# Loading the first tile of a row-norm kernel with two DMAs, one of the even and one of the odd partitions

## Chip, cores, metric

The kernel runs on one core of a Trainium2 chip. The metric is the device time of one execution in microseconds (us); lower is better. A profile is one execution; its span is some 1.8 us shorter than the device time.

## The reference

The input is 8192 x 8192 float32, 268 MB; the output is the largest absolute value of each row.

```python
def reference(x):
    return np.linalg.norm(x, ord=np.inf, axis=1)
```

Every byte is read once and reduced once, so the time cannot fall below that of the reading.

## The kernel before

The first 6144 rows go through as 24 tiles of 128 partitions with 64 KB each (two rows of the matrix per partition), with three buffers. The last rows are cut into smaller loads so that little work is left after the last byte. All loads are issued by SyncE (SP in the profile); VectorE (DVE) reduces.

```python
for a in range(A):                 # A = 6
    for n in range(G):             # G = 4
        t = sbuf.tile([P, W + PAD], F32, tag="t")      # 3 buffers, W = 16384
        nc.sync.dma_start(out=t[:, :W], in_=x_b[a, n])
        absmax(
            r_bulk[:, a, n * B : (n + 1) * B],
            t[:, :W].rearrange("p (b c) -> p b c", b=B),
        )
# ... 34 smaller loads and their reduces, two stores ...
nc.at_finalize(start_first_load_early)
nc.at_finalize(finish_on_pool)
```

`start_first_load_early` moves the first DMA of SyncE, and only that one, to the head of the program, before the start-up barrier of the engines. This move is called the hoist below:

```python
if ins.engine == sp and type(ins).__name__ == "InstDMACopy":
    assert not ins.sync_info.on_wait
    # ... taken out of its block and put in front of SyncE's first instruction
    return
```

Of the kernel before, what the change touches and what calls it, by code (L numbers as in the profile page):

```python
# [34 lines left out]
def segments(loads, cols):  # L35

    out, at = [], 0
    for i, w in enumerate(loads):
        end = at + w
        while at < end:  # L40
            r = at // cols
            to = min(end, (r + 1) * cols)
            out.append((i, r, at - r * cols, to - at))
            at = to
    return out
# [53 lines left out]
@with_exitstack  # L99
def kernel(  # L100
    ctx: ExitStack,
    tc: tile.TileContext,
    x: bass.AP,
    out: bass.AP,
    G: int = 4,
    B: int = 2,
    BUFS: int = 3,
    PAD: int = 16,
):
    nc = tc.nc  # L110
    P = nc.NUM_PARTITIONS
    rows, cols = x.shape
    W = B * cols


    n_tail = B * (len(TAIL) + 1)
    n_bulk_rows = rows // P - n_tail
    assert n_bulk_rows % (G * B) == 0
    A = n_bulk_rows // (G * B)
    split = n_bulk_rows * P  # L120
    x_b = x[:split].rearrange("(a p n b) c -> a n p (b c)", p=P, a=A, n=G, b=B)
    out_b = out[:split].rearrange("(a p n b) -> p a (n b)", p=P, a=A, n=G, b=B)
    x_t = x[split:].rearrange("(p t b) c -> t p (b c)", p=P, b=B)
    out_t = out[split:].rearrange("(p t) -> p t", p=P)

    sbuf = ctx.enter_context(tc.tile_pool(name="sbuf", bufs=BUFS))
    outp = ctx.enter_context(tc.tile_pool(name="outp", bufs=1))

    segs = [segments(loads, cols) for loads in TAIL]
    k_max = max(sum(r == b for _, r, _, _ in s) for s in segs for b in range(B))  # L130
    parts_of = [sum(r == b for r, _ in LAST) - 1 for b in range(B)]
    assert sum(parts_of) <= PAD

    r_bulk = outp.tile([P, A, G * B], F32)
    r_tail = outp.tile([P, n_tail], F32)
    part = outp.tile([P, n_tail - B, k_max], F32)
    nc.vector.memset(part[:], 0.0)  # L137

    def absmax(o, i):
        return nc.vector.reduce_max(  # L140
            out=o, in_=i, axis=X, apply_absolute_value=True
        )

    for a in range(A):
        for n in range(G):
            t = sbuf.tile([P, W + PAD], F32, tag="t")
            nc.sync.dma_start(out=t[:, :W], in_=x_b[a, n])
            absmax(
                r_bulk[:, a, n * B : (n + 1) * B],
                t[:, :W].rearrange("p (b c) -> p b c", b=B),  # L150
            )

    for i, loads in enumerate(TAIL):
        t = sbuf.tile([P, W + PAD], F32, tag="t")
        todo = segs[i]
        seen = [0] * B
        at = 0
        for j, w in enumerate(loads):
            nc.sync.dma_start(out=t[:, at : at + w], in_=x_t[i][:, at : at + w])  # L159
            at += w  # L160
            for _, b, c, n in [s for s in todo if s[0] == j]:
                k, lo = seen[b], b * cols + c
                absmax(part[:, i * B + b, k : k + 1], t[:, lo : lo + n])
                seen[b] += 1

    def after(ins, first, kind):
        info = mybir.DependencyInfo(kind, mybir.DependencyReason.SCHED_ONLY)
        tc.add_manual_dep(ins.ins, first.ins.name, info, reason="order")


    t = sbuf.tile([P, W + PAD], F32, tag="t")
    left = parts_of[:]
    col = [0] * B
    at, slot = 0, {}
    ends = [w for _, w in LAST[-B:]]
    lo = W - sum(ends)
    for b in range(B):
        slot[b] = lo + ends[b]
        lo = slot[b] + parts_of[b]
    for j, (b, w) in enumerate(LAST):  # L180
        final = left[b] == 0
        to = slot[b] - w if final else at
        frm = b * cols + col[b]
        nc.sync.dma_start(out=t[:, to : to + w], in_=x_t[len(TAIL)][:, frm : frm + w])
        col[b] += w
        if final:
            r = n_tail - B + b
            absmax(r_tail[:, r : r + 1], t[:, to : slot[b] + parts_of[b]])
        else:
            left[b] -= 1  # L190
            k = slot[b] + left[b]
            done = absmax(t[:, k : k + 1], t[:, to : to + w])
            at += w
        if j == 0:

            ins = absmax(r_tail[:, : n_tail - B], part[:])
            after(ins, done, mybir.DependencyClass.NoSync)
        if j == len(LAST) - 4:

            ins = nc.scalar.dma_start(out=out_b, in_=r_bulk[:])  # L200
            after(ins, done, mybir.DependencyClass.Sync)
    nc.sync.dma_start(out=out_t, in_=r_tail[:])
    nc.at_finalize(start_first_load_early)
    nc.at_finalize(finish_on_pool)
# [30 lines left out]
```

## Time and profile before

| | before |
|---|---|
| device time, median of 3 | 627.47 us (627.43 to 627.56) |
| span of the profile | 625.7 us |
| DMA rate over the span | 429 GB/s |
| one full tile of 8.39 MB | 19.35 us |
| VectorE busy | 552.9 us, 88% |
| first reduce begins | 21.99 us |

The prediction below shows the lines for most of this and reads them: the kernel is as long as the start of a stream of loads, the stream, and a short tail. Three words are used all through. A packet is one record of a DMA engine at work; for the big tiles it is one row of 64 KB. The completion write is the 4-byte record, of 0.009 us, that each of the 16 engines shows at the end of its part of a load (944 of them in SyncE's queue, for 58 loads and a store). A tile is called landed here when the last of the 16 is written.

From the timeline of the kernel before (start us, length us, queue, line, operation): the first load is issued in 0.38 us.

```profile
0.00 0.38 SPq L147 DMA_DIRECT2D t<-in_x_dram  x1
```

The view of the load's source line, with shortest, median and longest issue in ns over its 24 loads: an issue of 128 rows usually takes 0.328 us. (The longest, 0.632, is the third, which follows directly on the second.)

```profile
L147 SPq DMA_DIRECT2D t<-in_x_dram x24: 327/328/632, 0.0 to 425.9; - x24
```

### The profile page before, as it was taken

What the parts mean: (1) busy time and instruction counts of PE and PEld (TensorE: products, weight loads), DVE (VectorE), ACT (ScalarE), POOL (GpSimd) and SP (SyncE); (2) the same over time, 40 slices, a digit from 0 to 9 for tenths busy, and PEclk for the clock granted to TensorE, in tenths of its full rate; (3) what the DMA queues carried; (4) which work ended last, traced back from release to release, by engine and by line L of the source; (5) the groups of instructions that cost most, each with busy time, mean ns of one, the idle gap of its engine ahead of it and who ended that gap; (6) DMA issues with size and microseconds to landing.
All of it is one profiled execution on the core that took longest, in us unless ns stands there. A gap on an engine that the chain in (4) does not pass through costs nothing.

```text
span 625.7 us, 205 instructions
## 1 busy us (share of the span) xinstructions
DVE 552.9 (88%) x67; POOL 0.2 (0%) x4
## 2 busy tenths in 40 slices
DVE  0588988889988889888898888988889999999998
POOL 0000000000000000000000000000000000000000
DMA  9999999999999999999999999999999999999997
GB/s 402 469 402 452 419 452 419 448 423 436 436 419 452 411 461 402 469 402 469 402 469 402 461 411 452 419 448 423 444 413 421 444 425 431 436 425 430 424 422 315
DMA packets 9282, 268.49 MB, mean 429 GB/s; under 512 B 1856, under 2 KB 1856, under 8 KB 3392
## 3 DMA queue, kind: packets, MB, share of 16 engines
q1 hardware_dynamic: 8496, 268.45, 99.5%
q10 hardware_dynamic: 784, 0.02, 0.1%
q14 instruction: 2, 0.02, 0.0%
HBM read 268.44 MB, written 0.03 MB: 429 GB/s over the span
## 4 chain that ended last, share of the span: by engine, by line
DMA 67%; DVE 31%; issue 1%; another core or an unknown queue 0%; DVEq 0%; SPq 0%
DMA t<-in_x_dram 67%; DVE r_bulk L140 24%; DVE part L140 6%; DVE t L140 2%; DVEq L230 0%; DVE r_tail L140 0%; SPq L159 0%
## 5 line engine op out<-in xcount | busy, mean ns | idle before, releaser
L140 DVE TENSOR_REDUCE r_bulk<-t 128x2 f32<-128x16384 f32 x24 | 413.3, 17220 | 69.7 <-DMA t<-in_x_dram 69.7
L140 DVE TENSOR_REDUCE part<-t 128x1 f32<-128x8192 f32 (+20 forms) x28 | 121.5, 4410 | 0.3 <-DMA t<-in_x_dram 0.3
L140 DVE TENSOR_REDUCE t<-t 128x1 f32<-128x1664 f32 (+8 forms) x11 | 16.7, 1576 | 0.2 <-DMA t<-in_x_dram 0.2
L140 DVE TENSOR_REDUCE r_tail<-t 128x1 f32<-128x644 f32 (+1 forms) x2 | 1.5, 814 | 0.0
L137 DVE MEMSET part<- 128x56 f32 x1 | 0.1, 105 | 0.9 <-PEq L219 0.9
L140 DVE TENSOR_REDUCE r_tail<-part 128x14 f32<-128x56 f32 x1 | 0.2, 201 | 0.0
L219 POOL MEMSET const-bfloat16-1.0<- 128x1 bf16 x1 | 0.1, 101 | 0.0
L219 POOL MEMSET const-uint8-127<- 128x1 uint8 x1 | 0.1, 101 | 0.0
L219 POOL MEMSET const-float32-0.0<- 128x1 f32 x1 | 0.1, 98 | 0.2 <-issue 0.2
L219 POOL MEMSET const-float32-1.0<- 128x1 f32 x1 | 0.1, 98 | 0.0
## 6 DMA issues: line engine op xcount, KB each, us to landing
t<-in_x_dram SPq DMA_DIRECT2D x2, 3392.0 KB, 37.2
t<-in_x_dram SPq DMA_DIRECT2D x1, 5376.0 KB, 40.5
t<-in_x_dram SPq DMA_DIRECT2D x1, 4864.0 KB, 32.9
t<-in_x_dram SPq DMA_DIRECT2D x1, 4800.0 KB, 32.9
t<-in_x_dram SPq DMA_DIRECT2D x1, 4672.0 KB, 34.7
t<-in_x_dram SPq DMA_DIRECT2D x3, 1536.0 KB, 36.9
t<-in_x_dram SPq DMA_DIRECT2D x1, 3520.0 KB, 42.7
t<-in_x_dram SPq DMA_DIRECT2D x1, 3328.0 KB, 40.4
```

Of the source, the lines that this page charges most:

```text
L137: nc.vector.memset(part[:], 0.0)
L140: return nc.vector.reduce_max(out=o, in_=i, axis=X, apply_absolute_value=True)
L219: nc = _bacc.Bacc("TRN2", target_bir_lowering=False, num_devices=1)
```

## The change

The first load is what is issued first and what the whole stream stands behind. The change issues it as two loads of 64 partitions each. As the text of the change gives no reason, the intent is inferred: a smaller first DMA might be under way sooner.

```diff
             t = sbuf.tile([P, W + PAD], F32, tag="t")
-            nc.sync.dma_start(out=t[:, :W], in_=x_b[a, n])
+
+            step = 2 if a == n == 0 else 1
+            for k in range(step):
+                nc.sync.dma_start(out=t[k::step, :W], in_=x_b[a, n][k::step, :])
             absmax(
```

With a step of 1 the other 23 loads are what they were. The early-start pass moves only the even half.

## The prediction

> **What bounds the kernel now.** I read the page from the top: engine busy time, the DMA row over the span, the bytes, then the chain of waits, the waits of VectorE and of the issuing queue, and last the first microseconds in narrow windows.
>
> First the page's busy shares of the DMA engines over 40 slices and the bytes:
>
> ```profile
> span 625.7 us, 205 instructions
> DMA  9999999999999999999999999999999999999997
> ...
> HBM read 268.44 MB, written 0.03 MB: 429 GB/s over the span
> ```
>
> The DMA row is at 9 in every slice but the last. VectorE does much less than the span: its costliest group takes 17.22 us for a tile, and each time stands idle before it for a DMA:
>
> ```profile
> L140 DVE TENSOR_REDUCE r_bulk<-t 128x2 f32<-128x16384 f32 x24 | 413.3, 17220 | 69.7 <-DMA t<-in_x_dram 69.7
> ```
>
> The chain that ended last, in order of time, shows the period. (One step is called "an unknown queue"; it is the wait for a load.)
>
> ```profile
> 0.79 40.47 DMA t<-in_x_dram
> ...
> 60.64 17.23 DVE r_bulk L140
> 77.87 0.02 issue
> 77.89 40.76 DMA t<-in_x_dram
> 118.65 0.02 issue
> 118.67 17.23 DVE r_bulk L140
> 135.91 0.02 issue
> 135.92 40.77 DMA t<-in_x_dram
> ```
>
> Three tiles take 135.91 - 77.87 = 58.04 us, 19.35 us each. A tile is 128 rows of 64 KB, 8.39 MB, so 8.39 MB / 19.35 us = 434 GB/s. The chain passes through VectorE only because a reduce gives a buffer back. A load is then asked for with about two tiles (40.76 us) still ahead of its landing, so the queue never runs dry. This is a stream bounded by the DMA engines. The trace's records of single packets say the same: a 64 KB packet takes 2.418 us almost without exception. 8 rows on each of 16 engines make 8 x 2.418 = 19.34 us, the period. Everything after the first load is that stream; what can move is when it begins and how the first 8 MB flow.
>
> The first microseconds, in windows (columns: length, VectorE, GpSimd, clock, DMA share, GB/s; a packet's bytes stand in the window in which it starts):
>
> ```profile
> 0.50:1.00 0.50, 0.10 (x1) 0.00 (x0) 1.00 0.00 0
> 1.00:1.20 0.20, 0.00 (x0) 0.00 (x0) 1.00 9.39 3277
> 1.20:1.40 0.20, 0.00 (x0) 0.00 (x0) 1.00 1.90 655
> 1.40:1.60 0.20, 0.00 (x0) 0.00 (x0) 1.00 1.98 655
> 1.60:1.80 0.20, 0.00 (x0) 0.00 (x0) 1.00 0.96 328
> 1.80:2.00 0.20, 0.00 (x0) 0.00 (x0) 1.00 0.90 328
> ```
>
> One 64 KB packet in 0.2 us is 328 GB/s, so these windows hold 10, 2, 2, 1 and 1 packets, 16 in all, one for each engine. The packet records give the first start at 1.01 us after the issue and the last at 1.82 us. Those first packets take 2.80 to 3.23 us in place of 2.42. The spread stays: the 16 completion writes of the first tile lie from 20.74 to 21.61 us (0.87 us apart), those of the 24th bulk tile from 465.32 to 466.22 (0.90), and a load near 604 us still 0.94. All engines carry equal shares at an equal pace, so whoever starts last lands last in every tile, nearly to the end.
>
> [...]
>
> **The change part by part.**
>
> - It removes one 128-row load and adds two 64-row loads of the same bytes: 64 + 64 packets of 64 KB, still 8 an engine. Data time: 8 x 2.418 = 19.34 us before and after. Sum: 0.
> - It adds one issue on the SyncE queue. An issue takes 0.33 us (the median of the 24 loads of the bulk; the longest took 0.63). By then the engines have the first half: 4 x 2.418 = 9.7 us of work, and the second half is asked for about 1 to 1.5 us in. Hidden, 0. The next two loads are issued 0.3 us later, with some 19 us of work ahead of them: 0.
> - It adds one completion write on each engine. A record of one takes 0.009 us, and the next row starts within 0.01 us of its due time. Sum: +0.01 us.
> - VectorE's first reduce has two completions to wait for; both belong to the same stream. [...] 0.
> - It moves the start. Only the first SyncE load is hoisted to the head of the program, and that is now half as large. If the 0.81 us between first and last engine (1.01 to 1.82) is the writing of descriptors engine after engine, half the descriptors need half the time: the last engine starts 0.4 us earlier and, as the spread is carried to the end, so does the end. If the spread is something else (cold first accesses: the late starters had the shorter first packets), the gain is 0. The late starters' second packets begin 0.89 us after the earliest, so most of the spread is real lateness. I choose somewhat over half: -0.28 us.
>
> Sum: 627.47 - 0.28 + 0.01 = 627.2 us. That is 0.04%, and far under the 2% line.
>
> **The rivals.**
>
> [...] every packet takes 2 x 2.418 = 4.84 us, each half 19.3 us in place of 9.7, and the first tile 38.7. As the stream is never idle later, the 19.3 us are never given back: 627.2 + 19.3 = 646.5 us, +3.0%, slower. [...] I give it 16%.
>
> *False order.* The two loads write one buffer. If their rows are taken as overlapping (0 to 126 against 1 to 127), the second half waits for the first to land. The stream would then start twice: the first tile's reduce began at 21.99 us, 21.99 - 19.34 = 2.65 us of start in it, and about that is added: 630 us, +0.4%, within 2%. Against: partition steps are part of an access, and a tracker that has them sees no overlap. 4%.
>
> *Hidden anyway.* The spread has a fixed cause, the start does not move: 627.4 to 627.6. For it: three of the five earliest starters had packets over 3.1 us, so a cold start may level what the earlier start wins. About 30%.
>
> **Range and chances.** Gain and hidden cases together have some 80%: 626.9 to 627.6, widened to 626.4 to 628.4 for a larger start effect (a whole 0.8 us gone) or a small cost of the extra load that I have overlooked. The conflict lies outside of the range, and so does the false order. Faster by 2% would need 12.5 us, nearly five times the whole start: 1%. Slower by 2% needs the conflict: 16%. Within: 83%.
>
> **What would show each step.** Right: the first reduce still waits for the load until 21.6 to 21.9 us (21.99 before); the first-tile packets at 2.42 us after the first; the windows of 1.0 to 2.0 us again with 16 packets, but closer together; the completion spread of all later tiles nearer to 0.5 than 0.87; the period still 19.35; the queue with one more issue and VectorE's 69.7 us of idle time changed by less than 1. Wrong by conflict: the first reduce at about 41 us, first-tile packets of 4.84 us, GB/s near 217 in the first two slices, VectorE's idle time up by 19. Wrong by false order: a gap of no packets near 11 us and the first reduce near 24.6. If neither shows and the time is off by over 1 us, something that I have not named moved the end of the stream.

The sum is 627.47 - 0.28 + 0.01 = 627.2 us; VectorE's further wait counted as 0 in it. The first rival supposes that every packet of the first tile takes twice its 2.418 us, and the text calls it the conflict. Other estimates rest on suppositions too. That 64 rows run on all 16 engines, 4 on each, the trace after shows; that the spread of 0.81 us is the writing of descriptors, or cold first accesses, no record shows.

## The result and the profile after

The changed kernel took 628.22 us in the median of 6 runs (627.84 to 628.80); the kernel before, in the same rounds, took 627.53 us (627.43 to 627.70). The ratio is 1.0011 with a 95% interval from 0.9998 to 1.0024, so by the 2% line it is the same. A ratio here is the mean time of one kernel's runs over that of the other's of the same rounds, and so not quite the ratio of the medians. The time lies in the stated range (626.4 to 628.4), but the small difference has the wrong sign: a gain of 0.28 us at the start, 0.27 in sum, was forecast, and the median rose by 0.69.

The page of the changed kernel shows a machine that does the same as before. The DMA row is unchanged, and so is the rate; one more load and one more wait of VectorE have joined the instructions; VectorE's idle time in front of its large reduces is 69.9 us in place of 69.7.

```profile
span 626.5 us, 207 instructions
...
DMA  9999999999999999999999999999999999999997
...
HBM read 268.44 MB, written 0.03 MB: 429 GB/s over the span
...
L140 DVE TENSOR_REDUCE r_bulk<-t 128x2 f32<-128x16384 f32 x24 | 413.3, 17220 | 69.9 <-DMA t<-in_x_dram 69.9
```

The timeline of the changed kernel tells how long SyncE took over its first issue, the even half, and when the first reduce began:

```profile
0.00 0.56 SPq L150 DMA_DIRECT2D t<-in_x_dram  x1
...
22.36 17.22 DVE L140 TENSOR_REDUCE r_bulk<-t 128x2 f32<-128x16384 f32 x1 [20.96 <-DMA t<-in_x_dram]
```

Half the rows took 0.56 us to issue where all of them took 0.38, and the first reduce began at 22.36 us, 0.37 later than before. The narrow windows of the changed kernel (length, VectorE, GpSimd, clock, DMA share, GB/s) show the same at the DMA engines:

```profile
1.00:1.20 0.20, 0.00 (x0) 0.00 (x0) 1.00 0.00 0
1.20:1.40 0.20, 0.10 (x1) 0.00 (x0) 1.00 3.85 1311
1.40:1.60 0.20, 0.00 (x0) 0.00 (x0) 1.00 6.61 2294
1.60:1.80 0.20, 0.00 (x0) 0.00 (x0) 1.00 1.97 655
1.80:2.00 0.20, 0.00 (x0) 0.00 (x0) 1.00 1.87 655
2.00:2.20 0.20, 0.00 (x0) 0.00 (x0) 1.00 0.92 328
```

At 328 GB/s a packet these are 0, 4, 7, 2, 2 and 1 packets. Before, ten packets started between 1.0 and 1.2 us; now none does. The records of single packets put the first at 1.35 us (1.01 before) and the last engine's first at 2.09 (1.82 before): both ends of the start moved later, by 0.33 and 0.27 us, and the spread between them shrank by only 0.07. Of the two ends only the first repeats: in further profiles the last engine's first packet came at 2.40 us before, and at 2.01 and 2.14 with the change.

The chain that ended last, in order of time, has a new link, the issue of the second half, and then the old rhythm:

```profile
1.21 0.48 SPq L150
1.69 0.05 issue
1.74 39.85 DMA t<-in_x_dram
...
78.23 0.02 issue
78.25 40.87 DMA t<-in_x_dram
119.11 0.02 issue
119.13 17.23 DVE r_bulk L140
136.37 0.02 issue
136.38 40.80 DMA t<-in_x_dram
```

The new link need not cost time: when the second half has been issued, at 1.69 us, the engines have 4 rows of the first half each, over 9 us of work (4 x 2.418 = 9.7; the completion writes of the first half lie from 11.57 to 12.27 us). Three tiles take 136.37 - 78.23 = 58.14 us against 58.04 before, a tenth of a microsecond more in this stretch.

Where did the 0.7 us come in? The last engine's completion write dates each landing. The first tile landed 0.32 us later than before (21.93 against 21.61), the 24th bulk tile 0.69 later (466.91 against 466.22), the last load 0.72 later (623.38 against 622.66). So 0.32 us come from the start, and 0.37 from the stream up to the 24th tile, in which 165 of the 64 KB packets took over 2.44 us, 149 of them between 40 and 250 us; before, none did. Their excess over 2.418 us sums to 0.50 us for each of 16 engines. The first part looked like the change itself, the second might be chance. The experiments had to tell these apart.

### The profile page after: what moved, and what is told of

Same layout as the page of the kernel before. It is cut to its first block, busy times and chain, and to the rows that moved or that the text cites. A ratio compares the mean times of both kernels' runs of the same rounds, so it can differ in the third digit from the quotient of the medians. Undisturbed runs are those within 1.5% of the kernel's fastest.

```text
span 626.5 us, 207 instructions
## 1 busy us (share of the span) xinstructions
DVE 553.0 (88%) x67; POOL 0.2 (0%) x4
## 4 chain that ended last, share of the span: by engine, by line
DMA 67%; DVE 31%; issue 1%; another core or an unknown queue 0%; DVEq 0%; SPq 0%
DMA t<-in_x_dram 67%; DVE r_bulk L140 24%; DVE part L140 6%; DVE t L140 2%; DVEq L233 0%; DVE r_tail L140 0%; SPq L150 0%; SPq L162 0%
## 5 line engine op out<-in xcount | busy, mean ns | idle before, releaser
L140 DVE TENSOR_REDUCE r_bulk<-t 128x2 f32<-128x16384 f32 x24 | 413.3, 17220 | 69.9 <-DMA t<-in_x_dram 69.9
```

Of the source, the lines that this page charges most:

```text
L140: return nc.vector.reduce_max(out=o, in_=i, axis=X, apply_absolute_value=True)
```

## The experiments

**The changed kernel again.** No edit.

> The changed kernel again. Theory A (the first issue of the strided half takes longer, so the first packet starts 0.33 us later and the whole stream with it; the rest of the loss is chance in the stream): 627.8 to 628.1 us, 0.3 to 0.6 above the kernel before, with the part over 0.33 varying from run to run. Theory B (the whole +0.7 us belongs to the change): 628.2 us again, +0.7 in most runs. Rival C (no difference at all, the first six runs were chance): within 0.1 us of before. In the profile all three expect the first packet at about 1.35 us if the late start is real.

Measured: 627.90 us in the median of 5 (627.84 to 628.86) against 627.55 (9 runs, 627.40 to 628.21); ratio 1.0008, interval 0.9995 to 1.0022. The first issue took 0.56 us again, the first packet came at 1.34 us, the first reduce began at 22.40. This fits theory A: about 0.33 us from the start are there again, and the part above it is smaller. The profile had 85 slow packets (over 2.44 us), half as many as the first.

**Contiguous halves.**

```diff
+            step = 2 if a == n == 0 else 1
+            for k in range(step):
+                p = slice(k * P // step, (k + 1) * P // step)
+                nc.sync.dma_start(out=t[p, :W], in_=x_b[a, n][p, :])
```

> The first tile in two contiguous halves, partitions 0 to 63 and 64 to 127. [...] its packets take about 4.84 us and the first tile lands about 19 us later: 646 to 647 us. If the packets stay at 2.42 us, 627.5 to 628.2. The length of the first issue tells what made it 0.56 us in the changed kernel (0.38 before): about 0.56 if it is the count of 64 rows, about 0.38 or less if it is the step of 2.

Measured: 649.01 us (4 runs, 648.91 to 649.10), 21.5 us above before and 2 us more than expected; ratio 1.0341, interval 1.0327 to 1.0355, slower. Windows of this kernel, with the same columns:

```profile
24.00:40.00 16.00, 0.00 (x0) 0.00 (x0) 1.00 0.96 197
44.00:60.00 16.00, 16.00 (x1) 0.00 (x0) 1.00 1.06 459
```

Between 24 and 40 us, in the second half of the first tile, the rate is 197 GB/s; from 44 us on it is back at the level of before (442 GB/s in the same window there). Its page shows VectorE's idle time up by 20.8 us in the same group, which comes before the first reduce (it begins at 43.61 us in place of 21.99):

```profile
L140 DVE TENSOR_REDUCE r_bulk<-t 128x2 f32<-128x16384 f32 x24 | 413.3, 17220 | 90.5 <-DMA t<-in_x_dram 90.5
```

In the records, the packets after the first take about 5.12 us in place of 2.42; so 16 engines move 16 x 65,536 B / 5.12 us = 205 GB/s, and the 197 of the window, which counts whole packets, is a little low. A packet takes 2.1 times as long here, about what the prediction feared for the even and odd split, in another split; the 5.12 in place of the expected 4.84, eight times over, make about the 2 us. What slows these packets no record shows. In the changed kernel all packets after an engine's first stay at 2.42 to 2.6 us: nothing there takes twice as long. The first issue of this kernel, with 64 adjacent rows, took 0.56 us too:

```profile
0.00 0.56 SPq L150 DMA_DIRECT2D t<-in_x_dram  x1
```

So the longer issue does not need the step of two; the count of 64 rows is enough. First packet: 1.34 us.

**Halves of the columns.**

```diff
+            step = 2 if a == n == 0 else 1
+            for k in range(step):
+                c = slice(k * W // step, (k + 1) * W // step)
+                nc.sync.dma_start(out=t[:, c], in_=x_b[a, n][:, c])
```

> The first tile in two loads of all 128 partitions, half of the columns each. Theory A (step or row count slows the first issue, not the number of loads): first issue 0.38 us, first packet at 1.01 us, time that of the kernel before within 0.1 us. Rival (two loads in place of one cost the time as such): +0.3 to +0.7 us as with even and odd.

Measured: first issue 0.37 us and first packet at 1.00 us, as theory A expected. Two loads in place of one therefore cost no start. The first tile even landed at 21.44 us, 0.17 earlier than before, with a spread of 0.52 us between engines in place of 0.87. But the time was 627.89 us (5 runs, 627.70 to 628.25) against 627.55, not within 0.1 as expected: a miss. In time alone the rival (+0.3 to +0.7 for two loads as such) did better than theory A, although no start was late. It is taken up again below.

**All tiles but the first in even and odd halves.**

```diff
-            step = 2 if a == n == 0 else 1
+            step = 1 if a == n == 0 else 2
```

(This is against the changed kernel.)

> The first tile whole, the other 23 tiles as even and odd halves. Theory A (the cost lies in the start alone): start as before (first packet at 1.01 us) and the time of the kernel before within 0.2 us, because the longer issues are hidden behind full queues. Rival (halves slow the stream by themselves, by order of rows or by completion writes): at 0.37 us a split tile up to 23 x 0.37 = 8.5 us more, some 636 us.

Measured: 627.63 us (5 runs, 627.54 to 627.70) against 627.55; ratio 1.0001. Splitting the 23 tiles behind the first costs nothing that can be told from noise, so halves do not slow the stream by themselves. The view of the load's source line shows what the issues take, now over 46 loads of 64 rows and one of 128 (shortest, median, longest in ns):

```profile
L149 SPq DMA_DIRECT2D t<-in_x_dram x47: 388/597/704, 0.0 to 426.5; - x47
```

The median of 0.597 us is not the price of 64 rows alone. From 39 us on, the first half of each tile takes 0.47 us and the second, which follows directly on it, 0.60, as the timeline shows for one tile:

```profile
77.97 0.47 SPq L149 DMA_DIRECT2D t<-in_x_dram  x1
...
78.48 0.60 SPq L149 DMA_DIRECT2D t<-in_x_dram  x1
```

The fair comparison is 0.47 for 64 rows with 0.33 for 128, where no issue stands just in front. SyncE pays 0.14 us more for half the rows, and more again for the second half, and the time does not show it.

**The hoist undone, without and with the change.** The edit is the same in both kernels:

```diff
-    nc.at_finalize(start_first_load_early)
```

> The kernel before, with the hoist of its first load undone, so that the load is issued behind the start-up barrier, some 0.45 us later (in the kernel before the second load is issued at 0.79 us, of which 0.38 are the first issue). If a late start passes to the end one for one: 627.95 to 628.1 us, 0.4 to 0.5 above before, with the first packet some 0.45 us after 1.01. If something later in the stream absorbs it: 627.5 to 627.6.

> The changed kernel with the hoist undone: both halves issued behind the barrier. If the half costs its own 0.33 us of start wherever it is issued, 0.3 to 0.4 us above the kernel before with the hoist undone, some 628.3 us. If the 0.33 us come from being hoisted (a cold sequencer, the barrier), no more than that kernel, some 628.0 us.

Measured: 628.29 us (5 runs, 628.14 to 628.39) without the change, 628.68 us (4 runs, 628.59 to 628.98) with it. Both lie above the times expected, but their difference lies where it was expected. The kernel before was itself slower and more scattered on the chip of these rounds, 628.05 us (9 runs, 627.43 to 628.45), so the comparison with it says little: a first packet 0.71 us later (1.73 against 1.01) showed as 0.24 us in the median. The comparison of the two late kernels is the useful one. Behind the barrier the changed one still takes 0.56 us over its first issue (0.37 without the change) and starts its first packet 0.35 us later (2.08 against 1.73), and its median is 0.39 us longer, with no overlap of the runs. Neither profile has more than one slow packet. So the late start of the half does not come from being hoisted, and here it is found again at the end.

**Quarters.**

```diff
-            step = 2 if a == n == 0 else 1
+            step = 4 if a == n == 0 else 1
```

> The first tile in four loads of 32 rows, four partitions apart. If the issue has a fixed longer form for anything but 128 rows, the first issue takes 0.5 to 0.6 us again and the time is that of the changed kernel, 627.8 to 628.2 us. If the issue grows as rows fall, over 0.7 us and a first packet after 1.5 us. If it falls with the rows, under 0.4. [...] packets after the first stay at 2.42 us; otherwise 4.8 to 5.1 us and over 640 us in all.

Measured: first issue 0.56 us, first packet at 1.33 us, packets after the first mostly at 2.42 to 2.44 us, 628.26 us (4 runs, 627.76 to 628.40), in the rounds in which the kernel before had 628.05. An issue of 32 rows takes as long as one of 64, 0.56 us, so between these two counts the extra neither grows nor falls with the rows. Nothing like the 5.12 us of the contiguous halves shows with rows four partitions apart either (the first reduce began at 22.57 us, not at 43.61).

**A small first load of all partitions.**

```diff
+            cuts = [0, 2048, W] if a == n == 0 else [0, W]
+            for lo, hi in zip(cuts, cuts[1:]):
+                nc.sync.dma_start(out=t[:, lo:hi], in_=x_b[a, n][:, lo:hi])
```

> The first tile in two loads of 128 rows, the first of 2048 columns (8 KB a row), the second of the rest. With halves of the columns the first tile landed 0.17 us earlier than before, with a spread of 0.52 between engines in place of 0.87, yet the time was not better. If smaller first packets level the engines' start, the first landing is at 21.3 to 21.5 us. The time then depends on which engine meets the two instruction fetches near 590 and 610 us: 627.4 to 627.9 us. If the landing does not come earlier, the spread is not set by the first packets.

Measured: first tile landed at 21.46 us with a spread of 0.53, as expected; 627.88 us (5 runs, 627.60 to 628.22) against 628.05 in the same rounds, ratio 0.9998. No gain that could be told from noise. Its profile had 162 slow packets.

**The kernel before, and the changed kernel, once more; and eight pieces of columns.** No edit for the first two; for the third the column cut above with `step = 8`.

> The kernel before under another name, for its scatter and a second profile of it. Its times should agree with those of the kernel before in the same rounds within 0.2 us of median. Theory A (engines that start further apart keep out of each other's way): a completion spread of the first tile near 0.87 us and no 64 KB packet over 2.44 us after the first 12 us. If slow packets are mere chance, or belong to the chip, some tens of them here as well.

> The changed kernel for a third profile. First issue 0.56 us, first packet at 1.34 us as twice before; 0.3 to 0.7 us above the kernel before of the same rounds in the median. Theory A: where the first-tile spread is under about 0.75 us, tens of slow packets between 40 and 250 us; where it is over 0.8, nearly none. A wide spread with many slow packets, or a tight one without any, speaks against A.

> The first tile in eight loads of 128 rows and 2048 columns. First issue 0.37 us and first packet at 1.0 us, as with the other column cuts; first tile landed at 21.4 to 21.5 us with a spread of about 0.5. Theory A expects over 20 slow packets again and a time of 627.6 to 628.0 us, no better than before by more than 0.1; if the earlier landing comes through, 627.3 to 627.4 us.

Measured: kernel before 627.50 us under its own name (9 runs) and 627.50 under the other (5 runs, 627.42 to 627.62). Changed kernel 627.82 us (5 runs, 627.74 to 627.94), +0.32; ratio 1.0005, interval 0.9992 to 1.0017. Eight pieces 627.93 us (5 runs, 627.88 to 628.39) against 627.50; ratio 1.0009, interval 0.9996 to 1.0021: landing at 21.65 us, later than expected, and no gain.

The packet records of the profiles, side by side. "Slow" counts 64 KB packets over 2.44 us that began after 24 us; times in us. (Left out are the contiguous halves, whose first tile is slow as a whole, and the two without the hoist and the quarters, which had at most 4 slow packets, at spreads of 0.86 to 1.01.)

| kernel | first packet | first tile landed | spread of that landing | slow packets | last load landed |
|---|---|---|---|---|---|
| before | 1.01 | 21.61 | 0.87 | 0 | 622.66 |
| before, second profile | 1.01 | 21.73 | 0.86 | 18 | 622.70 |
| changed | 1.35 | 21.93 | 0.71 | 165 | 623.38 |
| changed, second | 1.34 | 22.01 | 0.83 | 85 | 623.13 |
| changed, third | 1.36 | 22.27 | 1.14 | 0 | 622.98 |
| all but the first | 1.03 | 21.58 | 0.76 | 0 | 622.61 |
| column halves | 1.00 | 21.44 | 0.52 | 20 | 622.72 |
| small first columns | 1.00 | 21.46 | 0.53 | 162 | 623.26 |
| column eighths | 1.00 | 21.65 | 0.35 | 1 | 623.33 |

*Slow packets.* The theory in the last three expectations was that engines which start closer together get in each other's way. It falls: the tightest start of all, the eighths, had one slow packet, and the second profile of the kernel before had 18 at a spread of 0.86. They came in two of three profiles of the changed kernel, but also in kernels without the even and odd split: 162 with the small first columns, 20 with the column halves, 18 in the second profile of the kernel before. So they are not the change's own. What causes them stays open.

*The late start, averaged over the engines.* The table dates the last of 16 engines. The mean over all 16 is steadier. It lands the first tile at 21.16 and 21.19 us in the two profiles of the kernel before and at 21.50, 21.50 and 21.54 in the three of the changed one; the last load at 621.94 and 622.01 before, and at 622.71, 622.43 and 622.32 with the change. The third, without a slow packet, still carries the 0.3 us at the end; what the first two have on top is about what their slow packets cost (0.50 and 0.22 us for each engine). The late pair agrees: 21.83 and 22.19 at the first tile, 622.61 and 622.97 at the end. The column halves, at 21.16 and 621.96, are where the kernel before is. So the late start reaches the end in the profiles. Yet the profiled run of the column halves was the fastest of its five; why their median lay 0.34 us above before, as much as that of the changed kernel, no record shows.

*Why an earlier landing did not help.* The column cuts let the slowest engine finish the first tile earlier (0.17 us with halves) and yet ended no sooner. The records show one thing that meets a single engine: an 8 KB packet of the queue that the profile names "instruction" (called the fetch here; what it carries is in no record), two in the span (at 591.9 and 610.0 us before, at 588.0 and 610.2 with the change). It takes 0.31 us, and the packet behind it mostly takes some 0.4 us longer than its like (before, 0.87 us in place of 0.46), so that engine falls back by about 0.73 us for good. In the eighths it is seen in the list of the DMA queues for the window from 556 to 559 us (packets, MB, share of 16 engines):

```profile
q14 instruction: 1, 0.01, 0.6%
```

The completion writes of the 16 engines before it, in the eighths, lie 0 to 0.42 us behind the earliest; after it the engine that was at 0.38 is at 1.11, alone behind all the others, and each later landing is that much later. In the kernel before, the same fetch, at 591.9 us, met an engine that was 0.10 us behind the earliest. It came to stand at 0.82, still ahead of the latest at 0.92, and the landing did not move. (The second fetch, near 610 us, does move it there: the latest engine goes from 0.93 to 1.27.) An uneven start can thus hide such a hit if it falls on an early engine. The eighths lose in another way too: their packets of 8 KB take 0.309 us, so 64 of them take 19.8 us where 8 whole rows take 19.3, and the engines land the first tile at 21.54 us in the mean against 21.16. This reading of the records fits the six profiles that I followed through (before, changed, its second, all but the first, column halves and eighths), but no run took the fetch away, so as the cause of the lost gain it is argued and not shown.

## Why the prediction was right or wrong

The bound was right. The stream's period is the same with and without the change (58.14 and 58.04 us for three tiles), VectorE's idle time moved by 0.2 us, and the time stayed within 2%. That it also lies in the range is luck as far as the term of the start goes, which had the wrong sign: the range was 2 us wide, to leave room for a small overlooked cost among other things.

The conflict did not come: with even and odd rows the packets stayed at 2.42 to 2.6 us. Contiguous halves behave as it says. It was sized at 19.3 us, with packets of 4.84; measured in them were 21.5 us with packets of 5.12. How the rows of either split are dealt to the engines is in no record, so why the one doubles the packets' time and the other does not was not shown.

The false-order rival did not come either: the second half was issued at 1.21 us, long before the first landed. That each half runs on all 16 engines, with 4 rows each, held: the windows above show 16 first packets, and the trace has 16 completion writes more than before (960 against 944).

The part on the further issue held, though its terms were mis-sized. An issue was put at 0.33 us for a half; the second half took 0.48 us in the changed kernel. The next two loads were put 0.3 us later; they were issued at 1.74 and 2.40 us in place of 0.79 and 1.17. All of that is hidden behind the first half's packets, as said. The further wait of the first reduce, counted as 0, shows as 0.05 us in this profile and 0.01 in the second: from the landing to the reduce it was 0.43 us (21.93 to 22.36) and 0.39 (22.01 to 22.40), in place of 0.38 (21.61 to 21.99).

The step that failed is the last of the sum, in its words: "half the descriptors need half the time: the last engine starts 0.4 us earlier". The start is not set by a cost per row. The issue is 0.38 us with 128 rows, 0.56 with 64, adjacent or two apart, and 0.56 with 32. The first packet came at 1.33 to 1.36 us in place of 1.01 to 1.03, in every kernel whose hoisted first load has fewer than 128 rows, and at 1.00 when the first load has 128 rows and half of the bytes or an eighth. Nor did the spread fall by half, as it should if it were the writing of descriptors: from first to last engine the start took 0.67 to 0.79 us in three profiles of the changed kernel, and 0.81 and 1.39 in two before. So the term of -0.28 us should have been +0.33. Of these 0.33, the issue itself is 0.18 longer; where the other 0.15 between the end of the issue and the first packet come from is open. The rival called "hidden anyway" was right that the spread does not follow the rows, but no rival had the first packet come later. The prediction also misread two signs that it took for this rival: of the five earliest starters two and not three had packets over 3.1 us, and the late starters' first packets were no shorter (3.02 us in the mean for the later eight, 3.03 for the earlier).

In time all this is at the edge of what can be seen. Over three sets the changed kernel was 0.69, 0.35 and 0.32 us above before in the median; the last two have the size of the start. By time alone they could also be the cost of two loads as such, for the column halves lost 0.34 us without a late start; the late start rests on the packet records and on the late pair. No set's interval leaves out a ratio of 1, but 16 of 16 runs of the changed kernel were at 627.74 us or more, and only 3 of the 24 runs before in the same rounds. The slow packets in the first profile explain why the first set was worse, as far as one profile speaks for six runs.

"The spread is carried to the end" was half right. It is carried through 24 tiles, but the spread is also a reserve, as the fetch at 591.9 us shows: a delay that meets an early engine need not reach the end. That a gain which makes the engines even uses this reserve up is the reading above, argued and not shown.

## What to carry to other kernels

When a stream of full-size transfers bounds a kernel, splitting its first transfer can win no more than the start, and here the start got worse: the form that issued fastest was 128 partitions (0.36 to 0.39 us for the first load, against 0.56 with 64 or 32). No cut of the first load gained anything here, by columns neither; a cut by columns at least kept the early start. If partitions must be split, interleave the parts; even and odd cost 0.32 to 0.69 us here, 0 to 63 and 64 to 127 cost 21.5 us, more than a whole tile's time (19.35 us). Before you expect a smaller piece to start sooner, read from a trace what an issue of each form takes, and compare issues that stand alone with issues that stand alone.
